# The lower part of every second MLP weight tile: from an accumulating transfer instead of a DVE subtraction

## The chip, the cores and the metric

The kernel runs on one core of a Trainium2 chip. The metric is device time in microseconds (us) of one execution; the core's engines (TensorE, VectorE or DVE, ScalarE or ACT, GpSimd or POOL, SyncE or SP) run side by side, each through its own instructions in order, and wait for one another by semaphores. In the profile PE is TensorE's matmul and PEld its weight load. Sixteen transfer engines move data for all queues.

## What is computed

One layer on a sequence of 256 tokens and a width of 2048, all in float32:

```python
h = h + hybrid_mixer(rms_norm(h, norm_mix[l]), w_in[l], ...)
h = h + memory_cross_attention(rms_norm(h, norm_cross[l]), rms_norm(mem, mem_norm[l]), ...)
h = h + sqrelu_mlp(rms_norm(h, norm_mlp[l]), w_up[l], w_down[l])

def sqrelu_mlp(hn, w_up, w_down):            # w_up 2048 x 8192, w_down 8192 x 2048
    return jnp.square(jax.nn.relu(hn @ w_up)) @ w_down
```

The change lies in the last line alone, the MLP, which takes somewhat more than half of the time.

## The kernel before

TensorE multiplies in fp32r, a form of float32 with a shorter mantissa. To come near float32, each operand is split in two: an upper part `hi`, the value rounded to fp32r, and a lower part `lo`, the value less `hi`. A product is then `hi` with the activation's upper and lower part, and `lo` with its upper part.

**Weights.** All weights come as one stream of tiles, 128 x 1024 each, in the order in which they are used; tile numbers j count from the stream's start, and the MLP has the 256 tiles 194 to 449. Two tiles, an even and the odd one after it, are one load of 1 MB into one buffer `raw` (L239, issued by SP, which issues little else). There are three `raw` buffers (L154) and five each of `hi` and `lo` (L155). For each tile ACT copies `raw` to `hi`, which rounds (L248, in `w_hi`), and DVE subtracts `hi` from `raw` into `lo` (L259, in `w_lo`). Nothing else reads `raw`, so a buffer can be loaded again when both tiles in it have been split.

**Order.** Each engine's order is fixed when the program is built. `w_get(j)` (L264) is called when TensorE's work on tile j is written down; it writes down `hi` up to tile j+3 and `lo` up to tile j+2 (LOOK is 3), and the loads that follow. At run time the engines go ahead as far as buffers allow: `hi` of tile j uses the buffer of tile j-5. Evictions of finished sums are tasks, placed between these by a small model of the engines' times (`Sched`, L106; the constants in L249 and L260 are its estimates).

**MLP.** The hidden width is taken in four groups of 2048 features. In each, eight blocks of `w_up` and then eight of `w_down` run; a block is four weight tiles against all 2048 inputs and makes two sums in PSUM (`f_block`, L274). Per tile it has eight pairs of matmuls: `hi` with 512 columns (L293) and `lo` with 256 (L294). A block's two sums are evicted while the next block runs: ACT copies the half of a sum that came from the lower activations (`half`, L371), DVE adds the other (L373), and in the up blocks DVE squares what is positive and the result is split again (L1179 to L1186). The last block of all has its own function (`f_block_last`, L299): it takes its four tiles at once, and makes first the one sum over all four and then the other. Ahead of the MLP are eight short blocks of the attention's output (`wo_x`), whose evictions add to the residual H (L1143) and scale and split it for the MLP (L379, L381).

POOL has one transfer in the whole kernel (`ikT`, L559, 64 KB within SBUF) and no other work after the start.

Of the kernel before, what the change touches and what calls it, by code (L numbers as in the profile page):

```python
# [6 lines left out]
F32 = mybir.dt.float32  # L7
F32R = mybir.dt.float32r
U8 = mybir.dt.uint8
AF = mybir.ActivationFunctionType  # L10
OP = mybir.AluOpType
# [29 lines left out]
LOOK = 3  # L41
# [4 lines left out]
class Task:  # L46
# [22 lines left out]
    def act(self, n, ap=0, psum=False):  # L69
        s = self.s  # L70
        while s.act > s.pe + LIM or self.t > max(s.act, s.pe) + 0.2:
            yield
        s.act = max(s.act, self.t) + (0.06 if psum else 0.1) + n * 0.000833 + 0.093 * ap
        self.t = s.act + 0.15
# [75 lines left out]
def body(ctx, tc, nc, src, out):  # L150
# [9 lines left out]
    S_ = Sched()  # L160
# [23 lines left out]
    act = nc.scalar.activation  # L184
    V = nc.vector
# [42 lines left out]
    raw, hi, lo, hi_end = {}, {}, {}, {}  # L228
# [8 lines left out]
    def w_dma(upto):  # L237
        while state["dma"] <= min(upto, len(stream) - 1):
            nc.sync.dma_start(*raw_pair(state["dma"]))  # L239
            state["dma"] += 2  # L240

    def w_hi(upto):
        while state["hi"] <= min(upto, len(stream) - 1):
            j = state["hi"]
            w_dma(j)
            w = stream[j][1]
            hi[j] = wsplit.tile([P, 1024], F32R, tag="hi", name=f"hi{j}")
            act(hi[j][:, :w], raw[j][:, :w], AF.Copy)  # L248
            S_.act = max(S_.act, S_.pe) + 0.95  # L249
            hi_end[j] = S_.act  # L250
            state["hi"] += 1

    def w_lo(upto):
        while state["lo"] <= min(upto, len(stream) - 1):
            j = state["lo"]
            w_hi(j)
            w = stream[j][1]
            lo[j] = wsplit.tile([P, 1024], F32R, tag="lo", name=f"lo{j}")
            V.tensor_tensor(lo[j][:, :w], raw[j][:, :w], hi[j][:, :w].bitcast(F32), OP.subtract)  # L259
            S_.dve = max(S_.dve, S_.pe, hi_end.pop(j, 0.0) + 0.15) + 1.13  # L260
            state["lo"] += 1
            w_dma(state["lo"] // 2 * 2 + 4)

    def w_get(j):  # L264
        for k in (j - 1, j - 2):
            for d_ in (raw, hi, lo):
                d_.pop(k, None)
        w_lo(j)
        w_hi(j + LOOK)
        w_lo(j + LOOK - 1)  # L270
        return hi[j], lo[j]


    def f_block(j0, kts, ops, done, width=256, merged=False, mp=P, kpt=4, banks=None):  # L274

        nft = max(1, width // P)
        ps = banks or [mbank() for _ in range(nft)]
        for kt in range(kts):
            if kt % kpt == 0:
                wh, wl = w_get(j0 + kt // kpt)  # L280
            a, need = ops(kt)
            S_.need(*need)
            o = (kt % kpt) * width
            first, last = kt == 0, kt == kts - 1
            for f in range(nft):
                h_ = wh[:, o + f * P:o + f * P + mp]
                l_ = wl[:, o + f * P:o + f * P + mp]
                if merged:
                    mm(ps[f][:mp, :256], h_, a[:, :256], start=first, stop=False)  # L289
                    mm(ps[f][:mp, :256], h_, a[:, 256:], start=False, stop=False)  # L290
                    mm(ps[f][:mp, :256], l_, a[:, :256], start=False, stop=last)  # L291
                else:
                    mm(ps[f][:mp, :], h_, a, start=first, stop=False)  # L293
                    mm(ps[f][:mp, 256:], l_, a[:, :256], start=False, stop=last)  # L294
                S_.step(0.325)
                if last:
                    done(f, ps[f])

    def f_block_last(j0, ops, done):  # L299

        w = [w_get(j0 + i) for i in range(4)]
        for f in range(2):
            ps = mbank()
            for kt in range(KT):
                wh, wl = w[kt // 4]
                a, need = ops(kt)
                S_.need(*need)
                o = (kt % 4) * 256 + f * P
                mm(ps[:, :256], wh[:, o:o + P], a[:, :256], start=kt == 0, stop=False)
                mm(ps[:, :256], wh[:, o:o + P], a[:, 256:], start=False, stop=False)  # L310
                mm(ps[:, :256], wl[:, o:o + P], a[:, :256], start=False, stop=kt == KT - 1)  # L311
                S_.step(0.325)
            done(f, ps)

    def t_block(j0, ops, done):

        ps = [mbank() for _ in range(2)]
        for kt in range(KT):
            if kt % 2 == 0:
                wh, wl = w_get(j0 + kt // 2)  # L320
            a, need = ops(kt)
            S_.need(*need)
            o = (kt % 2) * 512
            first, last = kt == 0, kt == KT - 1
            for t in range(2):
                xh = a[:, t * P:t * P + P]
                xl = a[:, 256 + t * P:256 + t * P + P]
                mm(ps[t], xh, wh[:, o:o + 512], start=first, stop=False)  # L328
                mm(ps[t], xh, wl[:, o:o + 512], start=False, stop=False)  # L329
                mm(ps[t], xl, wh[:, o:o + 512], start=False, stop=last)  # L330
                S_.step(0.65)
                if last:
                    done(t, ps[t])
# [85 lines left out]
    i_mlp = []  # L419
# [211 lines left out]
    for kt in range(KT):  # L631
        if kt in (4, 8):
            start_split(kt // 4 + 1)
            state["hi"] = state["lo"] = kt // 2 + 4
        a = A[kt]
        for b in range(2):
            wh, wl = hi[kt // 4 * 2 + b], lo[kt // 4 * 2 + b]
            for f in range(2):
                o = (kt % 4) * 256 + f * P
                ps = bank4[2 * b + f]  # L640
                mm(ps, wh[:, o:o + P], a, start=kt == 0, stop=False)  # L641
                mm(ps[:, 256:], wl[:, o:o + P], a[:, :256], start=False, stop=kt == KT - 1)  # L642
                S_.step(0.325)
                if kt == KT - 1:
                    iq_done(b)(f, ps)
        if kt >= 12:
            w_lo(kt - 4)
# [695 lines left out]
```

## Time and profile before

| | us |
|---|---|
| median of the runs | 1331.79 (1331.66 to 1331.92) |
| the profiled execution | 1332.08 |
| its span, first to last instruction | 1330.1 |
| TensorE busy in it | 1323.8 |
| DVE busy | 895.9 |
| ACT busy | 659.3 |
| POOL busy | 0.8 |

The trace is of one execution. "Busy" counts an engine's instructions and not what it waits for; matmuls are pipelined, and their single times overlap. In lists of waits, the engine and line on the left waited for those on the right. In a timeline, brackets give the idle time ahead of an instruction and what ended it. Shares of the transfer engines are means over all sixteen.

### The profile page before, as it was taken

How to read it: one execution, taken by the hardware profiler on the slowest of the kernel's cores; microseconds unless marked ns; L12 is line 12 of the kernel's file. 1: busy time of each engine (PE TensorE's matmuls, PEld its weight loads, DVE VectorE, ACT ScalarE, POOL GpSimd, SP SyncE). 2: the span in 40 equal slices, each digit the busy share in tenths (PEclk: the TensorE clock that was granted, in tenths of full speed). 3: DMA queues.
4: the chain of work that ended last, by engine and by line, in shares of the span. 5: the costliest groups of instructions: out<-in, count | busy, mean ns of one | idle time of the engine just before them, and what ended most of it. 6: DMA issues, size and time to landing. Idle time of an engine off the chain costs nothing.

```text
span 1330.1 us, 18650 instructions
## 1 busy us (share of the span) xinstructions
PE 1323.8 (100%) x7396; PEld 1144.8 (86%) x7396; DVE 895.9 (67%) x1523; ACT 659.3 (50%) x982; POOL 0.8 (0%) x5
## 2 busy tenths in 40 slices
PE   9999999999999999999999999999999999999999
PEld 7888888888888888889888888888888888888888
DVE  7797988656566768669765445665556655597653
ACT  7545434345675557667444444444444444444442
POOL 0000000000000000000000000000000000000000
PEclk9999999999999999999999999999999999999999
DMA  9444534545435556535555554555555555555562
GB/s 335 161 162 164 182 131 151 192 160 190 158 132 186 186 179 220 211 127 186 190 190 191 193 188 188 190 190 190 190 190 190 190 190 190 190 190 190 205 214 88
DMA packets 38711, 244.12 MB, mean 184 GB/s; under 512 B 4432, under 2 KB 6480, under 8 KB 10464
## 3 DMA queue, kind: packets, MB, share of 16 engines
q1 hardware_dynamic: 37584, 239.75, 49.6%
q10 hardware_dynamic: 1008, 3.12, 0.6%
q8 instruction: 58, 0.95, 0.3%
q14 instruction: 29, 0.24, 0.1%
q0 software_dynamic: 32, 0.07, 0.0%
HBM read 240.75 MB, written 2.10 MB: 183 GB/s over the span
## 4 chain that ended last, share of the span: by engine, by line
PE 97%; DVE 2%; DMA 1%; ACT 0%; issue 0%; DVEq 0%
PE m L293 45%; PE m L294 22%; PE m L328 7%; PE m L330 7%; PE m L329 7%; PE m L641 1%; PE s L741 1%; PE m L642 1%; PE m L290 1%; PE m L291 1%; PE m L289 1%; DMA slot<-in_memT_dram 0%; DVE lo L259 0%; PE s L916 0%; PE s L586 0%; PE m L311 0%
## 5 line engine op out<-in xcount | busy, mean ns | idle before, releaser
L293 PE MATMUL m<-slot,hi 128*128 128x512 f32 x2592 | 905.6, 395 | 0.0
L294 PE MATMUL m<-slot,lo 128*128 128x256 f32 x2592 | 720.3, 278 | 0.1
L293 PEld LDWEIGHTS m<-slot,hi 128*128 128x128 f32 x2592 | 486.2, 188 | 114.5
L259 DVE TENSOR_TENSOR lo<-raw,hi 128x1024 fp32r<-128x1024 f32 (+1 forms) x442 | 528.0, 1219 | 72.3 <-ACT hi L248 72.3
L248 ACT ACTIVATE hi<-raw 128x1024 fp32r<-128x1024 f32 (+1 forms) x442 | 465.4, 1055 | 180.4 <-PE m L293 112.4
L294 PEld LDWEIGHTS m<-slot,lo 128*128 128x128 f32 x2592 | 487.1, 188 | 0.5 <-DVE lo L259 0.5
L371 ACT ACTIVATE half<-m 128x256 f32<-128x256 f32 x166 | 62.8, 379 | 327.9 <-PE m L294 327.1
L373 DVE TENSOR_TENSOR z<-m,half 128x256 f32<-128x256 f32 x150 | 63.5, 424 | 207.1 <-ACT half L371 207.0
L328 PE MATMUL m<-hi,slot 128*128 128x512 f32 x416 | 169.7, 408 | 0.0
L330 PE MATMUL m<-hi,slot 128*128 128x512 f32 x416 | 162.7, 391 | 0.0
L329 PE MATMUL m<-lo,slot 128*128 128x512 f32 x416 | 162.3, 390 | 0.3 <-DVE lo L259 0.3
L330 PEld LDWEIGHTS m<-hi,slot 128*128 128x128 f32 x416 | 78.1, 188 | 17.0
L329 PEld LDWEIGHTS m<-lo,slot 128*128 128x128 f32 x416 | 78.4, 188 | 14.4 <-DVE lo L259 0.7
L328 PEld LDWEIGHTS m<-hi,slot 128*128 128x128 f32 x416 | 78.3, 188 | 13.8
L747 DVE COPY_PREDICATED slot<-lmask,s 128x192 f32<-128x192 uint8 (+2 forms) x72 | 25.0, 349 | 14.7 <-PE s L741 13.1
L373 DVE TENSOR_TENSOR slot<-m,half 128x256 f32<-128x256 f32 x16 | 6.8, 425 | 33.6 <-ACT half L371 33.6
L1179 DVE SCALAR_TENSOR_TENSOR sg<-z 128x256 f32<-128x256 f32 x64 | 27.2, 425 | 2.1
L1184 ACT ACTIVATE slot<-sg 128x256 fp32r<-128x256 f32 x64 | 26.5, 413 | 2.6 <-DVE sg L1182 2.1
L1186 DVE TENSOR_TENSOR slot<-sg,slot 128x256 fp32r<-128x256 f32 x64 | 26.8, 419 | 0.0
L641 PE MATMUL m<-slot,hi 128*128 128x512 f32 x64 | 22.8, 400 | 1.0 <-DVE slot L450 1.0
L387 DVE TENSOR_TENSOR slot<-s,slot 128x256 fp32r<-128x256 f32 (+1 forms) x16 | 7.9, 491 | 21.1 <-ACT slot L385 21.1
L379 ACT ACTIVATE slot<-H,cst 128x256 fp32r<-128x256 f32 x32 | 16.3, 508 | 9.7 <-DVE H L1143 8.5
(198 smaller groups left out, 772.0 us busy)
## 6 DMA issues: line engine op xcount, KB each, us to landing
raw<-in_w_up_dram SPq DMA_DIRECT2D x64, 1024.0 KB, 4.9
raw<-in_w_down_dram SPq DMA_DIRECT2D x64, 1024.0 KB, 5.1
raw<-in_w_qf_dram SPq DMA_DIRECT2D x16, 1024.0 KB, 4.8
raw<-in_w_out_dram SPq DMA_DIRECT2D x16, 1024.0 KB, 4.8
raw<-in_w_ti_dram SPq DMA_DIRECT2D x8, 1024.0 KB, 5.0
raw<-in_w_tv_dram SPq DMA_DIRECT2D x8, 1024.0 KB, 4.9
raw<-in_w_tk_dram SPq DMA_DIRECT2D x8, 1024.0 KB, 4.8
raw<-in_w_tq_dram SPq DMA_DIRECT2D x8, 1024.0 KB, 4.8
```

Of the source, the lines that this page charges most:

```text
L248: act(hi[j][:, :w], raw[j][:, :w], AF.Copy)
L259: V.tensor_tensor(lo[j][:, :w], raw[j][:, :w], hi[j][:, :w].bitcast(F32), OP.subtract)
L293: mm(ps[f][:mp, :], h_, a, start=first, stop=False)
L294: mm(ps[f][:mp, 256:], l_, a[:, :256], start=False, stop=last)
L328: mm(ps[t], xh, wh[:, o:o + 512], start=first, stop=False)
L329: mm(ps[t], xh, wl[:, o:o + 512], start=False, stop=False)
L330: mm(ps[t], xl, wh[:, o:o + 512], start=False, stop=last)
L371: act(h, ps[:, 256:], AF.Copy)
L373: V.tensor_tensor(dst, ps[:, :256], h, OP.add)
L641: mm(ps, wh[:, o:o + P], a, start=kt == 0, stop=False)
L1179: V.scalar_tensor_tensor(r, z, 0.0, z, op0=OP.max, op1=OP.mult)
L1186: V.tensor_tensor(dst[:, 256:], r, dst[:, :256].bitcast(F32), OP.subtract)
```

## The change

```diff
@@ w_lo @@
             lo[j] = wsplit.tile([P, 1024], F32R, tag="lo", name=f"lo{j}")
-            V.tensor_tensor(lo[j][:, :w], raw[j][:, :w], hi[j][:, :w].bitcast(F32), OP.subtract)
-            S_.dve = max(S_.dve, S_.pe, hi_end.pop(j, 0.0) + 0.15) + 1.13
+            if j >= i_mlp[0][0] and j % 2:
+                act(lo[j], raw[j], AF.Copy, scale=-1.0)
+                nc.gpsimd.dma_start(lo[j], raw[j], accum_op=OP.add)
+                S_.act = max(S_.act, S_.pe) + 0.95
+            else:
+                V.tensor_tensor(lo[j][:, :w], raw[j][:, :w], hi[j][:, :w].bitcast(F32), OP.subtract)
+                S_.dve = max(S_.dve, S_.pe, hi_end.pop(j, 0.0) + 0.15) + 1.13
             state["lo"] += 1
@@ w_get @@
         w_hi(j + LOOK)
-        w_lo(j + LOOK - 1)
+        w_lo(j + LOOK - (j < i_mlp[0][0]))
         return hi[j], lo[j]
```

For the odd tiles of the MLP, 128 of 256, ACT writes the negated rounded value into `lo`, and POOL issues a transfer that adds `raw` to it in place, within SBUF: 128 rows of 4 KB. The even tiles go as before. In the MLP `lo` is also written down one tile earlier, up to j+3 like `hi`. Lines behind the change move by five (L260 and L261 are the new copy and transfer, L264 the subtraction, L376 the eviction's copy, L384 and L479 what were L379 and L474).

ACT at the entry to the MLP; `hi`, `lo` and `raw` carry the tile's number first, and a `slot` written from H is a residual tile scaled for the MLP. Before:

```order
L248 ACTIVATE hi195_5529<-raw194_5342 128x1024
L379 ACTIVATE slot_444_5525<-H_99,cst_78 128x256
L379 ACTIVATE slot_447_5562<-H_99,cst_78 128x256
L248 ACTIVATE hi196_5566<-raw196_5418 128x1024
L379 ACTIVATE slot_447_5562<-H_99,cst_78 128x256
L379 ACTIVATE slot_450_5601<-H_99,cst_78 128x256
L248 ACTIVATE hi197_5610<-raw196_5418 128x1024
L379 ACTIVATE slot_450_5601<-H_99,cst_78 128x256
L248 ACTIVATE hi198_5634<-raw198_5494 128x1024
```

and now:

```order
L248 ACTIVATE hi195_5529<-raw194_5342 128x1024
L384 ACTIVATE slot_444_5525<-H_99,cst_78 128x256
L384 ACTIVATE slot_447_5562<-H_99,cst_78 128x256
L248 ACTIVATE hi196_5566<-raw196_5418 128x1024
L260 ACTIVATE lo195_5568<-raw194_5342 128x1024
L384 ACTIVATE slot_447_5562<-H_99,cst_78 128x256
L384 ACTIVATE slot_450_5602<-H_99,cst_78 128x256
L248 ACTIVATE hi197_5611<-raw196_5418 128x1024
L260 ACTIVATE lo197_5615<-raw196_5418 128x1024
L384 ACTIVATE slot_450_5602<-H_99,cst_78 128x256
L248 ACTIVATE hi198_5640<-raw198_5494 128x1024
```

The copies for tiles 195 and 197 have come in, the first behind `hi` of tile 196.

SP's loads in the middle of the MLP, with the engines and transfer queues that each waits for (DMASW is a transfer that POOL issued, DMAHW one of SP or ACT). Before:

```order
L239 DMA raw278_7529<-in_w_up_dram 128x2048 [waits DMAHW3_49,DVE_49,Activation_49]
L239 DMA raw280_7573<-in_w_up_dram 128x2048 [waits DMAHW4_49,DVE_49]
L239 DMA raw282_7632<-in_w_up_dram 128x2048 [waits DMAHW5_49,DVE_49,Activation_49]
L239 DMA raw284_7676<-in_w_up_dram 128x2048 [waits DMAHW6_49,DVE_49]
L239 DMA raw286_7735<-in_w_up_dram 128x2048 [waits DMAHW7_49,DVE_49,Activation_49]
```

and now:

```order
L239 DMA raw278_7541<-in_w_up_dram 128x2048 [waits DMASW0_49,DMAHW3_49,DVE_49,Activation_49]
L239 DMA raw280_7596<-in_w_up_dram 128x2048 [waits DMASW1_49,DMAHW4_49,DVE_49,Activation_49]
L239 DMA raw282_7646<-in_w_up_dram 128x2048 [waits DMASW2_49,DMAHW5_49,DVE_49,Activation_49]
L239 DMA raw284_7701<-in_w_up_dram 128x2048 [waits DMASW3_49,DMAHW6_49,DVE_49,Activation_49]
L239 DMA raw286_7751<-in_w_up_dram 128x2048 [waits DMASW4_49,DMAHW7_49,DVE_49,Activation_49]
```

Each load of the MLP now also waits for the accumulating transfer that reads its buffer.

ACT at the end of the kernel (446 to 449 are the last block's tiles; the `half` reading m_920 evicts the first sum of the block before it, which ends when the last block starts). Before:

```order
L248 ACTIVATE hi446_11874<-raw446_11778 128x1024
L248 ACTIVATE hi447_11894<-raw446_11778 128x1024
L248 ACTIVATE hi448_11914<-raw448_11820 128x1024
L371 ACTIVATE half_927_11935<-m_920_11841 128x256
L248 ACTIVATE hi449_11937<-raw448_11820 128x1024
L371 ACTIVATE half_930_11948<-m_921_11842 128x256
```

and now:

```order
L248 ACTIVATE hi446_12002<-raw446_11873 128x1024
L248 ACTIVATE hi447_12022<-raw446_11873 128x1024
L260 ACTIVATE lo447_12024<-raw446_11873 128x1024
L248 ACTIVATE hi448_12043<-raw448_11927 128x1024
L376 ACTIVATE half_927_12064<-m_920_11968 128x256
L248 ACTIVATE hi449_12066<-raw448_11927 128x1024
L260 ACTIVATE lo449_12068<-raw448_11927 128x1024
L376 ACTIVATE half_930_12076<-m_921_11969 128x256
```

Each odd tile's copy stands right behind its `hi`, and both of tile 449 stand behind the eviction of the block before, as `hi` did already.

## Rows read from the trace of the kernel before

**Rows 1.** Page, part 1: busy us (share of span) and instructions.

```profile
PE 1323.8 (100%) x7396; PEld 1144.8 (86%) x7396; DVE 895.9 (67%) x1523; ACT 659.3 (50%) x982; POOL 0.8 (0%) x5
```

**Rows 2.** Page, part 4: the chain that ended last, by engine.

```profile
PE 97%; DVE 2%; DMA 1%; ACT 0%; issue 0%; DVEq 0%
```

**Rows 3.** Two stretches: length, busy us (instructions) by engine; clock, transfer share, GB/s.

```profile
700.00:800.00 100.00, 100.00 (x579) 87.43 (x578) 51.14 (x59) 42.81 (x57) 0.00 (x0) 1.00 0.52 194
...
1100.00:1200.00 100.00, 100.00 (x579) 87.41 (x578) 71.23 (x116) 44.66 (x62) 0.00 (x0) 1.00 0.51 186
```

**Rows 4.** All waits of PE in the execution: us in total, times, longest.

```profile
PE s L200 <- DVE zero L197: 1.2, 1, 1.2
PE m L641 <- DVE slot L450: 1.0, 1, 1.0
PE m L329 <- DVE lo L259: 0.3, 1, 0.3
PE m L642 <- DVE lo L444: 0.2, 1, 0.2
```

**Rows 5.** Timeline of ACT in a down block: start us, us, instruction, [idle before].

```profile
1104.16 0.38 ACT L371 ACTIVATE half<-m 128x256 f32<-128x256 f32 x1 [4.25 <-PE m L294]
...
1107.16 1.06 ACT L248 ACTIVATE hi<-raw 128x1024 fp32r<-128x1024 f32 x1 [0.46 <-PE m L293]
1109.94 1.06 ACT L248 ACTIVATE hi<-raw 128x1024 fp32r<-128x1024 f32 x1 [1.71 <-PE m L293]
1115.25 0.38 ACT L371 ACTIVATE half<-m 128x256 f32<-128x256 f32 x1 [4.25 <-PE m L294]
```

**Rows 6.** Lines from 700 to 1300 us: busy us, mean ns | idle before.

```profile
L259 DVE TENSOR_TENSOR lo<-raw,hi 128x1024 fp32r<-128x1024 f32 x218 | 259.1, 1220 | 37.0 <-ACT hi L248 37.0
L248 ACT ACTIVATE hi<-raw 128x1024 fp32r<-128x1024 f32 x217 | 229.6, 1058 | 104.7 <-PE m L293 97.0 <-issue 5.7 <-ACT hi L248 2.0
...
L1184 ACT ACTIVATE slot<-sg 128x256 fp32r<-128x256 f32 x50 | 20.7, 413 | 2.1 <-DVE sg L1182 2.1
```

**Rows 7.** A stretch in which two loads follow each other, columns as in rows 3.

```profile
1011.00:1015.00 4.00, 4.00 (x25) 3.52 (x24) 1.23 (x1) 0.21 (x1) 0.00 (x0) 1.00 1.01 414
```

**Rows 8.** Tile ikT: POOL's one transfer (ns min/median/max), and its landing.

```profile
L559 POOL DMA_DIRECT2D ikT<-ikT x1: 638/638/638, 50.4 to 50.4; - x1
...
DMA to landing us min/median/max: 2.0/2.0/2.0
```

**Rows 9.** Tile raw, 700 to 1300 us: issue to landing of its loads.

```profile
DMA to landing us min/median/max: 4.7/5.1/7.2
```

**Rows 10.** Waits of SP's queue, 700 to 1300 us: total, times, longest.

```profile
SPq L239 <- DVE lo L259: 520.0, 109, 11.6
```

**Rows 11.** Timeline of PE at the entry to the MLP.

```profile
615.42 0.40 PE L293 MATMUL m<-slot,hi 128*128 128x512 f32 x1
...
618.25 0.40 PE L293 MATMUL m<-slot,hi 128*128 128x512 f32 x1
```

**Rows 12.** Timeline of ACT at the entry to the MLP.

```profile
613.25 1.04 ACT L248 ACTIVATE hi<-raw 128x1024 fp32r<-128x1024 f32 x1
...
616.13 1.04 ACT L248 ACTIVATE hi<-raw 128x1024 fp32r<-128x1024 f32 x1
617.98 0.51 ACT L379 ACTIVATE slot<-H,cst 128x256 fp32r<-128x256 f32 x1 [0.80 <-DVE H L1143]
618.40 1.05 ACT L248 ACTIVATE hi<-raw 128x1024 fp32r<-128x1024 f32 x1
```

**Rows 13.** Timeline of ACT at the start of the last block.

```profile
1314.93 0.38 ACT L371 ACTIVATE half<-m 128x256 f32<-128x256 f32 x1 [4.25 <-PE m L294]
1315.21 1.05 ACT L248 ACTIVATE hi<-raw 128x1024 fp32r<-128x1024 f32 x1
```

**Rows 14.** Timeline of DVE: the last block's two evictions.

```profile
1321.03 0.42 DVE L1196 TENSOR_TENSOR z<-m,slot 128x256 f32<-128x256 f32 x1 [1.92 <-PE m L311]
1326.78 0.42 DVE L1196 TENSOR_TENSOR z<-m,slot 128x256 f32<-128x256 f32 x1 [5.33 <-PE m L311]
```

## The prediction

> **What bounds the kernel now.** I read the page from the top: engines first, then the chain, then stretches, then single waits. TensorE is busy 1323.8 us of a span of 1330.1 us, DVE 895.9, ACT 659.3 [rows 1], and 97% of the chain that ended last is TensorE's own [rows 2]. By stretches, TensorE is busy for all of 700 to 800 us and of 1100 to 1200 us, with the clock granted in full [rows 3]. Its waits in the whole execution are four rows, 2.7 us together, the largest 1.2 us, and those on a `lo` tile 0.3 and 0.2 us [rows 4]. So in the MLP, where the change sits, TensorE waits for nothing, and DVE's work lies wholly beside it.
>
> The same two stretches settle whether TensorE would run faster beside an idler DVE: it starts 579 matmuls in either, with DVE busy 51.1 us in one and 71.2 us in the other [rows 3]. It would not.
>
> The MLP's beat: from one block's first eviction to the next is 1104.16 to 1115.25 us, 11.09 us for four weight tiles [rows 5]: 2.77 us a tile, 5.55 us a pair (one load). A split (`hi`) at 1107.16 and one at 1109.94 both ended a wait for a TensorE matmul [rows 5]: ACT waits for a buffer of the five, so `hi` of tile j starts when tile j-5 ends, four tiles (11.1 us) before tile j is due.
>
> **Removed.** 128 DVE subtractions of 1.22 us [rows 6], 156 us of DVE. DVE is not the bound, so this is worth 0 on the path.
>
> **Added on ACT.** 128 negated copies. No such row exists; the nearest is `hi`, the same copy without the factor, 1.06 us [rows 6]: 136 us. In a block ACT then has six of these and the evictions (two of 0.38 us [rows 5], and in an up block two more copies of 0.41 [rows 6]): some 8 us of 11.1. It fits. The cover is ACT's idle time; without it each copy would cost its 1.06 us.
>
> **Added on the transfer engines.** 128 accumulating transfers of 512 KB, issued by POOL, which has nothing else queued in the MLP. Each must read the raw part and the negated part and write one. No row shows an accumulation. Where two loads follow each other without pause, the engines move 414 GB/s at full share [rows 7], 2.53 us for a 1 MB load. Bounds for the accumulation's time on the engines: 1.26 us if only its 512 KB count at that rate; 3.8 us if two reads and a write follow one another (1.5 MB). I take two reads with the write beside them, 2.53 us, since a load too has a read and a write and runs at one rate. Per pair: 2.53 + 2.53 = 5.06 us of 5.55, 91%. It fits, with little room; an accumulation over 3.0 us does not.
>
> The Trainium skill (Collectives: The Full Stack, section "The bandwidth ceiling: the fold count and why AG ≠ RS ≠ AR") says the add in the transfer engine costs nothing by itself, and that a reduction runs at half a copy's rate for its two source reads, from about 31 GB/s per engine. By that the accumulation would take an estimated 2.1 us and the pair 4.6 of 5.55 us; the verdict would be the same. No run here shows it yet.
>
> **The new wait.** From issue to landing, call it L. One POOL transfer exists, 64 KB within SBUF: 0.64 us on POOL and 2.0 us to landing, so 1.84 us besides its 0.16 us of data [rows 8]. With 2.53 us of data L is 4.4 us. From the other side: a 1 MB load lands after 5.1 us (4.7 to 7.2) [rows 9]; with POOL's 0.64 us that is 5.7, and 7.8 from the longest. The floor is 1.84 + 1.26 = 3.1 us. I take 5.5, nearer the loads, since the engines are shared.
>
> Who waits? First TensorE, for `lo`: `hi` and the negated copy end 2.2 us after `hi` may start, and the tile is due at 11.1, so L may be 8.9. Second SP: it issues only loads, and a raw buffer is now free when the accumulation has landed, not when DVE has subtracted (SP's wait now, 109 times, 520 us, harmless [rows 10]). A buffer's round is load + `hi` + `hi` + copy + hand-overs + L = 5.1 + 3.2 + 0.3 + L, and three buffers may take three pairs, 16.6 us: **load + L must stay under 13.1 us**. Mine is 10.6.
>
> **The two ends.** Here the lead is shorter. Entry: the MLP's first matmul is at 615.42 us, tile 195 begins 2.83 us later, at 618.25 [rows 11]. The copy for tile 195 stands behind `hi` of tile 196. In ACT's order the `hi` behind the last scaling of a residual tile (617.98 us) is that of tile 198, and so 618.40; two `hi` earlier, tile 196's is the one at 613.25 us [rows 12]. It ends at 614.3, the copy at 615.3, plus 5.5: 620.8, 2.5 us late. Tiles 197 and 199 have two and more tiles of lead again. Exit: the last block (its own function, L299) reads all four tiles for each half, so tile 449 is due after three quarters of the first half. The block starts near 1314.9, when the eviction before it stops waiting, and its halves end at 1321.03 and 1326.78, 5.75 us apart [rows 13, 14]; due at about 1319.2. `hi` of tile 449 stands behind that eviction, at 1315.21 [rows 13]; copy until 1317.2, plus 5.5: 1322.7, 3.5 us late. DVE made the deadline in both places.
>
> **Sum.** 0 (DVE) + 0 (ACT) + 0 (steady beat) + 2.5 + 3.5 = +6 us. The profiled execution took 1332.08 us, span 1330.1 and 2 around it; the median shown is 0.3 lower. So 1331.8 + 6 = **1338 us**. Its own range is 1332 to 1350: L at its floor of 3.1 leaves a stall of under 2 us at the two ends together, L of 7.8 makes 2.3 + 2.3 more, and the rest is a beat that just misses.
>
> **Rivals.**
> *Loads and accumulations stretch each other (slower).* Both use the same engines, whose share in the MLP is 0.51 to 0.52 now [rows 3] and would be near 0.91; they would nearly always overlap. The longest landing of a load in the MLP, 7.2 us, shows what sharing does [rows 9]. If both took 7.2, load + L is 14.4, 1.3 us over the limit: 0.43 us a pair, 128 pairs, +55 us: with the ends about 1392. For it: the buffers' limit is close. Against: a load that starts when an accumulation lands tends to fall into the gap.
> The Trainium skill (DMA: Bandwidth & Descriptors, section "Issuing engines are not separate DMA queues") has the rule behind this: POOL's transfers run on the engines that the loads use. A separate queue buys no bandwidth.
>
> *The accumulation itself is slow (slower).* It decides from 3.0 us of engine time. At 3.8 us the pair takes 6.33, 0.79 over: 128 times, +101 us, 1438 with the ends. At twice my value, 5.06 us, it is 2.05 a pair, +262, 1600. For it: no row shows an accumulation, and a transfer with work in it may keep fewer bytes in flight. Against: nothing in the rows.
>
> *Faster.* At most the 6.3 us that TensorE is idle [rows 1], half of a per cent; the `lo` waits among them are 0.5 us. Excluded but for an unknown.
>
> **Chances.** Forecast (within 2%) 0.50; stretched 0.26, of which a tenth stays under 2%; slow accumulation 0.23; faster 0.01. Some 2%, or 27 us, is what a measurement here can tell from no change. Faster 0.01, same 0.53, slower 0.46. The range must take in the stretched case whole and the slow one at 3.8 us: 1332 + 101 + 50 = 1483, with what is slower still left out (about 0.15), and 1330 below. The point is the likeliest case.
>
> **What would show it.** Right: in the MLP TensorE stays busy in every stretch; the accumulations land within 4.4 to 6.5 us of their issue; SP waits for them and not DVE; two stalls on `lo`, at the MLP's first pair and in its last block; DVE down by some 156 us, ACT up by some 136. Wrong: the matmul on `lo` or its weight load (L294 of before) idle in each pair, 128 times, ended by a transfer: if the transfers' share is then near full, the slow accumulation; if it is well under full and ACT's `hi` waits for the load, the buffers' round.

## The result, and the profile after

The changed kernel takes 1376.48 us (1375.75 to 1377.21) against 1331.79 before: a ratio of 1.0336, interval 1.0319 to 1.0353. It is slower. The forecast of 1338 us, no change beyond 2%, was wrong; the time lies inside the range, near the rival of loads and accumulations that stretch each other, but, as the runs below show, only partly for that rival's reason.

The profiled execution has a span of 1374.0 us, 43.9 more than before. The page after: the engines as in [rows 1], two queues with packets, MB and share of sixteen engines' span, the chain as in [rows 2], two lines as in [rows 6], and two kinds of transfer with their number, KB each and median us from issue to landing:

```profile
PE 1343.7 (98%) x7396; PEld 1156.3 (84%) x7396; DVE 757.2 (55%) x1395; ACT 778.5 (57%) x1110; POOL 112.3 (8%) x133
...
q1 hardware_dynamic: 37584, 239.75, 47.3%
q0 software_dynamic: 18464, 67.18, 26.4%
...
PE 80%; DMA 11%; issue 8%; DVE 1%; ACT 0%; POOLq 0%
...
L261 POOL DMA_DIRECT2D lo<-raw x128 | 111.4, 870 | 1195.4 <-PE m L295 564.1
...
L260 ACT ACTIVATE lo<-raw 128x1024 fp32r<-128x1024 f32 x128 | 133.9, 1046 | 0.0
...
raw<-in_w_up_dram SPq DMA_DIRECT2D x64, 1024.0 KB, 5.7
lo<-raw POOLq DMA_DIRECT2D x128, 512.0 KB, 5.3
```

DVE has lost 138.7 us and ACT gained 119.2; the 128 new copies by themselves are 133.9 us. Queue q0, POOL's, took 26.4% of sixteen engines' span: over 128 accumulations 0.264 x 1374.0 / 128 = 2.8 us each. TensorE is busy 20 us longer, and its idle time has grown from 6.3 to 30.3 us; the chain has 11% of transfers in it where it had almost none [rows 2].

By stretches of the MLP (as [rows 3]: length, busy time and number of instructions for PE, PEld, DVE, ACT, POOL, then the granted clock, the transfer engines' share and GB/s):

```profile
700.00:800.00 100.00, 97.19 (x547) 84.60 (x546) 31.09 (x42) 57.19 (x73) 14.78 (x17) 0.98 0.96 271
1100.00:1200.00 100.00, 99.67 (x572) 87.39 (x572) 42.19 (x71) 59.20 (x74) 15.66 (x18) 1.00 0.99 283
```

In the same 100 us TensorE starts 547 and 572 matmuls where it started 579 in either [rows 3]. The transfer engines' share is 0.96 to 0.99, up from 0.51 and 0.52. The waits that end on a `lo` tile from the new transfer, and SP's waits (engine and line, what for: us in total, times, the longest):

```profile
PEld m L299 <- DMA lo<-raw: 31.1, 29, 3.6
PEld m L316 <- DMA lo<-raw: 2.6, 1, 2.6
...
PE m L299 <- DMA lo<-raw: 21.9, 21, 3.3
PE m L316 <- DMA lo<-raw: 2.4, 1, 2.4
```

```profile
SPq L239 <- DMA lo<-raw: 671.3, 125, 11.8
```

TensorE's 21.9 + 2.4 us answer to the 24.0 us of new idle time. So the new idle time is wholly `lo` tiles that come too late; its weight loads wait for them somewhat more often and longer, 33.7 us. SP's long wait for the accumulations passes on little: in the MLP ACT's `hi` waits for loads 42.8 us in 47 waits, and no wait of TensorE ends on a load.

Where in the block the tiles come late shows in ACT's and POOL's timelines (start us, duration, engine, line, operation; in brackets the idle time ahead and what ended it), here of one block and the start of the next:

```profile
1007.86 0.39 ACT L376 ACTIVATE half<-m 128x256 f32<-128x256 f32 x1 [4.21 <-PE m L299]
1008.14 1.05 ACT L248 ACTIVATE hi<-raw 128x1024 fp32r<-128x1024 f32 x1
1009.09 1.04 ACT L260 ACTIVATE lo<-raw 128x1024 fp32r<-128x1024 f32 x1
...
1018.95 0.39 ACT L376 ACTIVATE half<-m 128x256 f32<-128x256 f32 x1 [3.90 <-PE m L299]
```

```profile
1010.43 0.87 POOL L261 DMA_DIRECT2D lo<-raw  x1 [6.93 <-ACT half L376]
1014.15 0.87 POOL L261 DMA_DIRECT2D lo<-raw  x1 [2.85 <-ACT lo L260]
1021.52 0.87 POOL L261 DMA_DIRECT2D lo<-raw  x1 [6.50 <-ACT half L376]
```

And TensorE in the second of the two blocks:

```profile
1028.96 0.39 PE L299 MATMUL m<-slot,lo 128*128 128x256 f32 x1 [1.15 <-DMA lo<-raw]
```

`half` is the first eviction of the block before; it waits for TensorE, so its start marks the new block's. Behind it in ACT's order stand `hi` and the negated copy of the block's **fourth** tile, and so the accumulation is issued some 2.6 us after the block began (1007.86 to 1010.43, 1018.95 to 1021.52). It starts 0.3 us after the copy's end, 1010.13; the `half` in POOL's brackets is the next one on ACT, which happens to end in between. The fourth tile is due after three tiles, 3 x 2.77 = 8.3 us: its transfer has 5.7 us. The second accumulation of each block, 3.7 us later, is for the next block's second tile, due 2.77 us into it, and has 7.6 us (1014.15 to 1021.7). But for the wait at the MLP's entry, all of TensorE's stalls inside blocks end 9.0 to 11.8 us after their block's first `half`, that is at the fourth tile; the one shown ends 10.0 us after it. None is at a second tile. The transfers of fourth tiles take 5.9 us from issue to landing in the median, a quarter of them over 6.8, those of second tiles 5.1.

### The profile page after: what moved, and what is told of

The parts are those of the page before. It is cut to its first block, busy times and chain, and to the rows that moved or that the text cites. A ratio compares the mean times of both kernels' runs of the same rounds, so it can differ in the third digit from the quotient of the medians.

```text
span 1374.0 us, 19298 instructions
## 1 busy us (share of the span) xinstructions
PE 1343.7 (98%) x7396; PEld 1156.3 (84%) x7396; DVE 757.2 (55%) x1395; ACT 778.5 (57%) x1110; POOL 112.3 (8%) x133
## 3 DMA queue, kind: packets, MB, share of 16 engines
q0 software_dynamic: 18464, 67.18, 26.4%
## 4 chain that ended last, share of the span: by engine, by line
PE 80%; DMA 11%; issue 8%; DVE 1%; ACT 0%; POOLq 0%
PE m L298 33%; PE m L299 18%; DMA lo<-raw 10%; PE m L333 7%; PE m L335 7%; PE m L334 7%; PE m L646 1%; PE s L746 1%; PE m L647 1%; PE s L921 0%; PE m L296 0%; PE m L295 0%; PE m L294 0%; PE s L591 0%; DMA cst<-in_consts_dram 0%
## 5 line engine op out<-in xcount | busy, mean ns | idle before, releaser
L298 PE MATMUL m<-slot,hi 128*128 128x512 f32 x2592 | 916.5, 397 | 0.0
L299 PE MATMUL m<-slot,lo 128*128 128x256 f32 x2592 | 732.2, 282 | 22.3 <-DMA lo<-raw 21.9
L299 PEld LDWEIGHTS m<-slot,lo 128*128 128x128 f32 x2592 | 492.4, 190 | 31.8 <-DMA lo<-raw 31.1
L264 DVE TENSOR_TENSOR lo<-raw,hi 128x1024 fp32r<-128x1024 f32 (+1 forms) x314 | 380.1, 1221 | 189.2 <-ACT hi L248 188.4
L376 ACT ACTIVATE half<-m 128x256 f32<-128x256 f32 x166 | 62.8, 379 | 317.7 <-PE m L299 316.5
L261 POOL DMA_DIRECT2D lo<-raw x128 | 111.4, 870 | 1195.4 <-PE m L295 564.1
L260 ACT ACTIVATE lo<-raw 128x1024 fp32r<-128x1024 f32 x128 | 133.9, 1046 | 0.0
L333 PEld LDWEIGHTS m<-hi,slot 128*128 128x128 f32 x416 | 78.3, 188 | 13.7
L646 PE MATMUL m<-slot,hi 128*128 128x512 f32 x64 | 22.9, 400 | 0.8 <-DVE slot L455 0.8
```

What stands on the lines that cost most here:

```text
L260: act(lo[j], raw[j], AF.Copy, scale=-1.0)
L261: nc.gpsimd.dma_start(lo[j], raw[j], accum_op=OP.add)
L376: act(h, ps[:, 256:], AF.Copy)
```

## The experiments

Two theories stood against each other. By the first, **the lead is too short**: the accumulation is as quick as predicted, but the fourth tile of each block is asked for too late by the order on ACT. By the second, **sharing stretches everything**: with the transfer engines near full, accumulations and loads take longer, and the round of the three `raw` buffers no longer closes. The changes below are against the changed kernel; before was 1331.5 to 1332.2 us beside them, and each ratio is to before. Remarks behind # in the cuts of code name the run and do not stand in the kernel. Traces are of one execution of each, which need not be the median one.

### Half as many accumulations

Only the block's fourth tile by the transfer (64 of them), and then only its second:

```diff
-            if j >= i_mlp[0][0] and j % 2:
+            if j >= i_mlp[0][0] and j % 4 == 1:      # late_only
+            if j >= i_mlp[0][0] and j % 4 == 3:      # early_only
```

> Only the fourth tile of each block (64 of the 128), the one whose copy stands behind the eviction, comes from a transfer; the second tile is subtracted by DVE. The transfer engines have half the accumulations, a share near 0.75. Theory 1 with a fixed L of 5.5 us or more: the stalls stay, 1350 to 1375 us. Theory 1 with L stretched by sharing: L falls to under 5 us, few stalls, 1334 to 1345 us. Theory 2: no stalls, 1333 us.

Measured: 1338.56 us, ratio 1.005 (1.0031 to 1.0068). A stretch of the MLP, the waits, and two of POOL's issues:

```profile
700.00:1300.00 600.00, 599.79 (x3436) 524.38 (x3435) 310.51 (x459) 310.25 (x425) 46.11 (x53) 1.00 0.74 236
```

```profile
PEld m L299 <- DMA lo<-raw: 2.6, 4, 0.9
PEld m L316 <- DMA lo<-raw: 2.6, 1, 2.6
```

```profile
908.31 0.87 POOL L261 DMA_DIRECT2D lo<-raw  x1 [10.22 <-ACT half L376]
919.40 0.87 POOL L261 DMA_DIRECT2D lo<-raw  x1 [10.22 <-ACT half L376]
```

The block's beat is 11.09 us here, as in [rows 5], and the issue stands exactly where it stood, 2.6 us into the block. The same tiles with the same lead of 5.7 us now hold it but for four: from issue to landing these transfers take 4.5 us at least, 4.6 in the median and 6.9 at most, against 4.6, 5.9 and 9.2 for the fourth tiles of the changed kernel. So the short lead alone is not enough; it takes a stretched transfer to miss it. The exit's stall stays, 2.6 us.

> The counterpart of late_only: only the second tile of each block (64 of 128), whose copy doesn't stand behind the eviction, comes from a transfer. Same transfers, same share of 0.75. Theory T: no stall in the blocks and none in the last block, whose fourth tile DVE makes again; 2.5 us at most at the entry: 1332 to 1336 us, and up to 14 us more if TensorE runs at its slower pace of 11.31 us a block, which has been seen in several of these runs. If the stalls came from sharing alone: as late_only, some 5 us.

Measured: 1343.7 us, ratio 1.0087 (1.0068 to 1.0107), and this was a miss for the theory of the lead: the second tiles have the longer lead, and yet

```profile
PEld m L299 <- DMA lo<-raw: 8.7, 12, 2.0
```

The transfers took 4.5, 5.7 and 10.1 us (least, median, most), more than the fourth tiles' in the run above at nearly the same share of the engines (0.76), and ACT's `hi` waited for loads 55.0 us in 26 waits. But for the one at the entry, the tiles that came late had not lost their lead: they had 7.6 to 10.0 us from issue to the turn of their first `lo` matmul (6.3 for the fourth tiles of the changed kernel, in the median), and their transfers took 8.3 to 10.1 us. So a stretched transfer can miss a long lead as well. Why these transfers are stretched more than those of the run above is open.

### What the add costs

The same number of transfers, the first as a plain copy, the second adding only the first 512 of 1024 columns (the rest of `lo` stays the negated upper part):

```diff
-                nc.gpsimd.dma_start(lo[j], raw[j], accum_op=OP.add)
+                nc.gpsimd.dma_start(lo[j].bitcast(F32), raw[j])                                # copyr
+                nc.gpsimd.dma_start(lo[j][:, :512], raw[j][:, :512], accum_op=OP.add)          # half
```

> The transfer copies raw over lo instead of adding to it, so for the odd tiles of the MLP the lower part is the whole weight: that part of the computation is changed. Order and count of all instructions the same. If an addition costs two reads at the load's rate (2.5 to 2.8 us of the engines), a copy costs 1.3 to 1.5 us, L falls by about 1.3 us to some 4 us, and both theories have 1332 to 1340 us. If the transfer's cost is by packet and not by bytes read, L and the time stay at 5.3 us and 1376 us.

Measured: 1360.24 us, ratio 1.0204 (1.0173 to 1.0235).

```profile
q0 software_dynamic: 18464, 67.18, 12.7%
```

```profile
PEld m L299 <- DMA lo<-raw: 19.4, 18, 2.3
```

A copy takes 0.127 x 1355.7 / 128 = 1.34 us of the engines, the accumulation 2.8, a factor of 2.1; beyond the second read little is left for the add (or for the output in fp32r, which the copy lacks). The Trainium skill has half a copy's rate for a reduction in the transfer engine, for its two source reads (Collectives: The Full Stack, "The bandwidth ceiling: the fold count and why AG ≠ RS ≠ AR"); the factor here agrees. The estimate of 2.1 us that the prediction worked out from its rate does not: 2.8 us were measured. Yet the kernel's time goes back by only a third of the loss. From issue to landing a copy still takes 4.4 us in the median, 2.9 at least and 8.2 at most, with the engines' share down to 0.78. So most of the way from issue to landing is not the add, and sharing stretches a transfer well below a full share.

> The accumulating transfer covers the first 512 of 1024 columns, so that in the odd MLP tiles the second half of lo stays the negated upper part: that part of the computation is left out. Order, instructions and waits as in the change; the engines' time of one accumulation falls from 2.8 to some 1.4 us, the share from 0.97 to about 0.78. Theory E (the transfer engines are full: 2.9 us for a load and 2.8 us for an accumulation against a pair's 5.55): with room to spare the stalls go, 1333 to 1340 us. Theory T (lead: every second accumulation has 5.7 us from issue to use and is stretched by the loads it meets): stalls stay in part, 1345 to 1362 us, as with the plain copy.

Measured: 1367.55 us, ratio 1.0273 (1.0239 to 1.0306). Half the bytes bring 9 us of 45: 3.3, 5.0 and 8.9 us from issue to landing (least, median, most), loads 6.1, TensorE busy 580.63 of 600 us from 700 to 1300, at a share of 0.80. ACT's `hi` waits for loads 88 us. Fewer bytes at the same moments do little.

### The lead

First the second part of the change alone is undone (`lo` written down one tile later again), then the lead is made longer (in the MLP `hi` and `lo` are written down one tile earlier, so that both stand ahead of `half`):

```diff
-        w_lo(j + LOOK - (j < i_mlp[0][0]))
+        w_lo(j + LOOK - 1)                           # lookback
```

```diff
-        w_hi(j + LOOK)
-        w_lo(j + LOOK - (j < i_mlp[0][0]))
+        mlp = j >= i_mlp[0][0]
+        w_hi(j + LOOK + mlp)                         # ahead
+        w_lo(j + LOOK - 1 + 2 * mlp)
```

> Of the change only the second part is undone: lo is again written down up to j+2 only, so that each copy stands one split further back on ACT. Transfers and bytes the same. Theory 1: the lead of an accumulation falls to about 5 us for the fourth tile and 5.7 us for the second, so that most of the 128 come late, by 0.5 to 1 us or more each: 1400 us or slower. Theory 2: the transfer engines have the same work, 1370 to 1385 us.

Measured: 1594.91 us in the median, single times from 1536 to 1657, so no interval is given; the trace is of the fastest, 1536.39 us. In it TensorE's weight loads wait 158.3 us on `lo` tiles of the blocks, up to 4.6 us each:

```profile
PEld m L299 <- DMA lo<-raw: 158.3, 76, 4.6
```

The accumulations take 5.1 us in the median, less than in the changed kernel, at a share of 0.82 from 700 to 1300 us; and yet this is some 160 us over the changed kernel even in the fastest execution. Not all of it is the lead: ACT's `hi` waits for loads 173.6 us. The second part of the change, `lo` one tile earlier, is what keeps its first part from costing far more.

> hi and lo of the MLP are written down one tile further ahead (up to j+4), so that the copy and the transfer of the block's fourth tile stand ahead of the eviction of the block before and not behind it. The transfers and their bytes are the same. Theory 1 (ACT's order: every second accumulation is issued 2.6 us after a block's start and has only 5.7 us until its tile is due, while it takes 5.6 to 8.9): the stalls on lo in the blocks go away, 1333 to 1340 us, with one stall of 2 to 3 us left at the entry. Theory 2 (the transfer engines are full and cannot deliver): share stays at 0.97 and so do the stalls, 1365 to 1385 us.

Measured: 1395.83 us, ratio 1.0499 (1.0451 to 1.0546): slower than the changed kernel, and a failure for the lead as the only cause. The waits:

```profile
ACT hi L248 <- DMA raw<-in_w_down_dram: 144.8, 58, 5.3
ACT hi L248 <- DMA raw<-in_w_up_dram: 113.8, 51, 7.2
PEld m L300 <- DMA lo<-raw: 44.6, 34, 2.9
```

ACT's `hi` now waits 258.6 us for loads, and the chain that ended last is 36% transfers. Loads land after 6.1 and 7.1 us (up and down weights), accumulations after 6.6 in the median: their sum of 12.7 to 13.7 us stands at the 13.1 us that the prediction gave the round of three buffers. So the second theory's limit is there as well, right behind the first. The longer lead did what it was meant to: of the 34 waits of weight loads only 5 are at fourth tiles, where the changed kernel has 28 of 29. The other 29 are at second tiles, whose transfers now take 8.6 us in the median instead of 5.1.

### Both at once

To move the second limit, first the half accumulation with the longer lead, then the longer lead with three accumulations in eight tiles, and then two versions with six `raw` buffers of one tile each, loaded by 512 KB transfers, in the changed kernel's order and with the longer lead:

```diff
+            if j >= i_mlp[0][0] and j % 8 in (3, 5, 7):          # three_ahead
```

```diff
-    wraw = pool("wraw", 3)
+    wraw = pool("wraw", 6)                                       # split, split_ahead
...
-            nc.sync.dma_start(*raw_pair(state["dma"]))
+            j = state["dma"]
+            w, ap = raw_pair(j)
+            nc.sync.dma_start(raw[j], ap[:, :w])
+            nc.sync.dma_start(raw[j + 1], ap[:, w:2 * w])
```

> As the half transfer (same part left out), and written down one tile further ahead, so that no copy stands behind an eviction. If lead and the engines' capacity are the two limits, both are now relieved: 1333 to 1338 us, with the entry's stall alone. If the further lookahead itself does harm (it was slower with whole accumulations), 1350 us or more.

Measured: 1346.38 us (single times 1337.85 to 1349.11), ratio 1.01 (1.0065 to 1.0136). The half accumulation gains 21 us by the longer lead, where the whole one lost 19.

```profile
700.00:1300.00 600.00, 600.00 (x3399) 520.32 (x3398) 242.84 (x404) 373.78 (x478) 92.23 (x106) 1.00 0.82 233
```

TensorE waits for nothing in 600 us, at full clock, and still makes only 3399 matmuls, against 3436 in the run with fourth tiles only and 3463 before. The last section comes back to this.

> One tile further ahead, and three of four odd tiles (96 of 128) accumulated whole, the fourth subtracted by DVE. Theory E: the engines need (2.9 + 0.75 x 2.8) / 5.55 = 0.90 of the time on the mean, which fits: 1335 to 1345 us. If the round of three raw buffers is the limit (load + L over 13.1 us while L is stretched to 7 us and more): still 1355 us or more.

Measured: 1367.63 us, ratio 1.0275 (1.0258 to 1.0293). With 96 accumulations and a share of 0.88 the round still doesn't close: `hi` waits 185.8 us for loads (6.3 and 6.4 us), accumulations take 6.9 us in the median, TensorE's weight loads wait 21.3 us on `lo`, in 18 of 20 waits at a second tile. Fewer bytes don't cure the round of two-tile buffers.

> The change as it is, in its own order, with the raw buffers of two tiles made six of one tile (loads of 512 KB). Theory T (lead: the copy behind the eviction leaves every second accumulation 5.7 us): the stalls on lo stay and the time is 1365 to 1385 us, since only the waits for loads go. Theory R (the buffers' round is what bounds the change itself): 1340 to 1355 us, as with the further lookahead.

Measured: 1416.38 us, ratio 1.0634 (1.0604 to 1.0664): no wait for an MLP load any more, and the worst of this group.

```profile
PEld m L302 <- DMA lo<-raw: 58.3, 43, 3.6
```

Loads now run as far ahead as they can, and the accumulations, with the short lead of 5.7 us, take 7.2 us in the median (4.6 to 10.7). Of the 43 waits 32 are at fourth tiles.

> One tile further ahead, all 128 accumulations, and the three raw buffers of two tiles made six of one tile, each with a load of its own of 512 KB, so that the even tile's buffer no longer waits for the accumulation. Bytes are the same. Theory R (the buffers' round is the limit): the wait for loads goes and the time falls from 1396 to 1340 or so. Theory E (engines full): share stays near 1 and the time stays at 1380 us or more.

Measured: 1352.7 us, ratio 1.0161 (1.0146 to 1.0176).

```profile
700.00:1300.00 600.00, 597.76 (x3384) 519.51 (x3383) 241.64 (x402) 368.93 (x475) 92.26 (x106) 1.00 1.01 279
```

```profile
PEld m L303 <- DMA lo<-raw: 7.3, 6, 2.7
```

The two factors make a square of four measured kernels:

| | two-tile buffers | one-tile buffers |
|---|---|---|
| changed kernel's order | 1376 | 1416 |
| longer lead | 1396 | 1353 |

Each change alone makes it slower, by 40 and by 19 us; both together make it 24 us faster. So neither theory stands alone. The accumulations of the last one take 7.2 us in the median, 1.9 more than in the changed kernel, and the share of the transfer engines is 1.01, yet TensorE hardly waits: with enough lead and free buffers a full share and slow transfers are hidden.

> One tile further ahead, buffers of one tile, and the first and the last two odd tiles of the MLP (195, 197, 447, 449) subtracted by DVE again, as where the lead is short by the program's order. Theory: lead and round are both relieved, the ends too; what is left is TensorE's pace: 1335 us at 11.09 us a block, 1349 us at 11.31. If whole accumulations still overload the engines, 1352 us as before.

The last version leaves the MLP's first and last four tiles to DVE:

```diff
-            if j >= i_mlp[0][0] and j % 2:
+            if i_mlp[0][0] + 4 <= j < len(stream) - 4 and j % 2:
```

Measured: 1344.14 us, ratio 1.0092 (1.0077 to 1.0107), 8.6 us less than without it; the waits on `lo` fall from 7.3 to 3.4 us. Not all of the 8.6 us are the ends. In the trace of the run before, 3.0 us are stalls in the MLP's first block; but 1.8 us are one at 1259 us, with some 1.7 us for the half clock behind it, and some 3 us a larger share of TensorE's slower pace (last section). A stretch of this run, with every odd tile accumulated, settles whether the transfer engines can carry it:

```profile
900.00:1000.00 100.00, 100.00 (x579) 88.19 (x578) 36.50 (x56) 60.92 (x75) 15.83 (x19) 1.00 1.02 286
```

They can: 579 matmuls as before [rows 3], at a share of 1.02. A share near one is not by itself a limit. No version was faster than before: DVE's time, which the change saves, was never on the path.

## Why the prediction was wrong, point by point

**DVE and ACT, 0 us: right.** 138.7 us less and 119.2 more (156 and 136 predicted; the copies alone 133.9), both beside TensorE's work.

**The accumulation's engine time: near, but the load's was short.** 2.8 us against 2.53 taken and 3.0 as the limit. A load was taken at 2.53 us too, while [rows 3] give it 0.52 x 5.55 = 2.9 us. So the two are 5.7 us of a pair's 5.55 rather than 5.06, and the limit of 3.0 was too generous; the share is 0.96 to 0.99 rather than 0.91. That the rival of a slow accumulation falls is shown not by this sum but by the stretch above, in which all pairs keep the beat.

**Issue to landing: right in the median, short in the spread.** 5.3 us against 5.5 taken; the longest, 9.8, is beyond my 7.8.

**The two ends, 2.5 and 3.5 us: right in place, and near in size.** The lists of waits give 2.4 us at the exit (last block, L316), and the timeline 1.70 at the entry:

```profile
620.28 0.38 PE L299 MATMUL m<-slot,lo 128*128 128x256 f32 x1 [1.70 <-DMA lo<-raw]
```

**"`hi` and the negated copy end 2.2 us after `hi` may start, and the tile is due at 11.1, so L may be 8.9": this is the step that failed, and with it the 0 for the steady beat.** I took the time at which the buffer allows `hi` for the time at which ACT does it. For the fourth tile of each block, half of all accumulations, `hi` and copy stand behind `half`, which waits for TensorE to finish the block before. Its lead is 8.3 - 2.6 = 5.7 us, not 8.9. The row was there. I read off the two `hi` of a block that wait for a buffer [rows 5], and passed over the other two, which stand behind `half` (the first right behind the `half` of 1104.16):

```profile
1104.44 1.05 ACT L248 ACTIVATE hi<-raw 128x1024 fp32r<-128x1024 f32 x1
...
1105.65 1.06 ACT L248 ACTIVATE hi<-raw 128x1024 fp32r<-128x1024 f32 x1
```

I saw this very order at the exit, for tile 449, and priced it; I did not ask whether every block has it. Against a lead of 5.7 us, L of 5.5 is no margin: by my own bounds of 4.4 to 7.8 a good part of 64 tiles had to come late. By the trace after, the fourth tiles' transfers take 5.9 us in the median and a quarter of them over 6.8; TensorE stands still at the fourth tiles of 20 of the 63 blocks before the last, 20.2 us, where the sum had 0.

**Stretching.** The rival was right that loads and accumulations stretch each other: 4.6 us with the 64 fourth tiles, 5.3 with 128, 7.2 where loads run freely; but 5.7 with the 64 second tiles, so the number alone does not decide it. Its condition, load + L over 13.1 us, is not met in the changed kernel (medians, 5.6 + 5.3 = 10.9), and its mark, ACT's waits for loads, is small there (42.8 us). It is about met with the longer lead (12.7 to 13.7), which gave 1396 us; that the rival's 1392 is so near is chance, as it was reckoned for another order. That the measured 1376 lies near it and inside the range is luck too: the range was widened for this rival and for the slow accumulation, and another cause brought the time there. What made the changed kernel slow is the short lead with enough stretch to miss it.

**What a stall costs.** I priced a stall at its own length. TensorE's idle time grew by 24.0 us, but the span by 43.9. A part of the rest is the clock. Behind the stall that ends at 640.57 us, 3.3 us long, 2.7 of them before 640, the granted clock is one half in the next stretch and 0.83 in the one after (columns as above):

```profile
635.00:640.00 5.00, 2.28 (x13) 1.72 (x12) 3.54 (x7) 4.35 (x5) 0.87 (x1) 0.99 1.01 226
640.00:645.00 5.00, 4.43 (x14) 3.85 (x15) 2.06 (x4) 0.00 (x0) 0.00 (x0) 0.50 1.03 300
645.00:650.00 5.00, 5.00 (x25) 4.33 (x25) 3.14 (x6) 4.97 (x9) 0.87 (x1) 0.83 0.71 247
650.00:655.00 5.00, 5.00 (x30) 4.36 (x29) 3.72 (x5) 2.09 (x3) 0.87 (x1) 1.00 0.87 153
```

That is the level of 1.2 instead of 2.4 GHz after a TensorE that had stood still for half of the stretch: 14 and 25 matmuls where 30 are started at the full clock. Such stretches, after the MLP's three longest stalls (3.3, 2.5 and 2.1 us) and the exit's (2.4), add up to some 17 us, half of which, 8.5 us, is lost (0.4 of it inside a stall). The starts of TensorE's matmuls in the two traces give the rest: a stalled tile and the one behind it together take 0.28 us more than the beat and the idle time, 5.8 us for 21 stalls; other tiles 2.5 us, mostly those in which weight loads wait for `lo` without an idle time of the matmuls (29 waits against 21); a slower pace of TensorE (below) some 3 us. With 21.9 and 2.4 us of idle time and 8.1 of the clock that makes 43.8.

## What to carry to other kernels

When an operation with a long way from start to end takes the place of a short one, read its start for every place in the repeating pattern from the engine's own order, with what stands ahead of it, and not from the moment at which its buffer comes free. Here the one tile of four with a short lead set the time for all, and a latency that varies has to fit by its tail, not its median. Then ask what the longer hold does to the buffers it reads: here lead and buffers had to be mended together, and either alone made things worse.

## What the runs showed of the hardware that I had not expected

**Half the engine time, little less latency.** The plain copy needs half the accumulation's engine time, and lands only 0.9 us earlier in the median. Both vary by a factor of two and more beside the loads: 4.6 to 9.8 us at a share of 0.96, 2.9 to 8.2 at 0.78.

**TensorE has two paces at one and the same granted clock.** With no wait at all and the clock at 1.00, one run makes a block in 11.3 us and another in 11.1. ACT's evictions (which start a block) in the half accumulation with the longer lead, and in the run with only the fourth tiles:

```profile
901.58 0.38 ACT L377 ACTIVATE half<-m 128x256 f32<-128x256 f32 x1 [0.53 <-PE m L300]
...
912.88 0.39 ACT L377 ACTIVATE half<-m 128x256 f32<-128x256 f32 x1 [0.58 <-PE m L300]
...
924.19 0.38 ACT L377 ACTIVATE half<-m 128x256 f32<-128x256 f32 x1 [0.58 <-PE m L300]
```

```profile
905.74 0.39 ACT L376 ACTIVATE half<-m 128x256 f32<-128x256 f32 x1 [4.26 <-PE m L299]
...
916.83 0.39 ACT L376 ACTIVATE half<-m 128x256 f32<-128x256 f32 x1 [4.26 <-PE m L299]
```

Periods of 11.30 and 11.31 us there, 11.09 here and before [rows 5]: 353 and 347 ns for a pair of matmuls, 2%, which over the MLP's 64 blocks would be 14 us. In the trace of the first of these runs 246 of 251 tiles go at the slower pace, 13 of the 16 us by which its span is longer than before. The kernel before has both paces too: its first MLP tile takes 2.83 us [rows 11], its steady beat gives 2.77. Most changes of pace come where TensorE's work is interrupted, but not all: in the changed kernel it slows at 1132 us and quickens at 1154, with no wait at either. The pace doesn't follow the transfers' share either: the run with only the fourth tiles goes at 11.31 us a block from 973 to 1173 us and at 11.09 from 760 to 960 and from 1180 to 1270, all at a share of 0.73 to 0.76. What selects it is open.
